# S5 in a decoder layer: a third accumulator bank, input copies by state tile, gates moved around the GLU, and the magnitudes and turns of the scan on VectorE in fewer, longer passes

## The chip, the cores and the metric

The kernel runs on one core of one Trainium2 chip. The metric is the device time of one execution in microseconds. Before the change the median of 3 runs is 1166.55 us (1165.32 to 1167.05).

## The reference, cut to what matters

One layer of a decoder over 288 tokens (256 of a prompt, and 8 samples of 4 new tokens each). One input projection feeds three branches and three sets of merge gates. Branch A is the one that the change is about: a diagonal complex state-space model (S5), then GELU, then a GLU.

```python
proj = x @ w_in                                   # 2048 -> xa, ga, ub, vb, gb, qkv, a, b, gate_c, zg
# branch A, 64 groups of 16 channels, 64 complex states each
bu = einsum('gpc,btgc->btgp', bb, u)              # bb from lam, dt, B
s  = associative_scan(s_t = a * s_(t-1) + bu_t)   # a = mag * exp(i * theta), complex
y  = Re(C s) + d * xa
z  = gelu(y);  z = z * sigmoid(z @ w_glu + b_glu)
pa = (z * silu(ga)) @ w_pa
g_a, g_b, g_c = sigmoid(zg + b_gate)
out = (g_a * pa + g_b * pb + g_c * pc) @ w_out
y = layernorm(ALPHA * x + out)
```

## The kernel before

All activations lie transposed, channels on partitions and 288 token columns along a row. Each weight matrix is streamed from memory once, in 322 pieces ("halves") of 128 x 1024 numbers. Each piece is loaded by SyncE's queue (`raw`), rounded to a high part on ScalarE (`wh`, line 203) and split from it on VectorE (`wl`, line 204 through the helper at line 136); `raw`, `wh` and `wl` have 3 buffers each. A product in full accuracy is three matmuls (high by high, low by high, high by low), so one half is 24 matmuls of 288 columns, all recorded at line 230.

The projections are jobs in a first-in-first-out list. `fill(n)` emits n units of 12 matmuls of that list, and the program calls it between the steps of the other work, so TensorE's order is the order of the calls. The other engines' orders are made by a scheduler; `tc.high_priority()` lifts some instructions ahead. Each job accumulates in one PSUM bank of the pool `ps_mm` (2 banks). The bank is free again when the job's result has been read: for a merge gate by the ScalarE tanh at line 1051 (`mth`), for a branch product by a VectorE pass.

S5 is worked in 8 blocks (n) of 128 channels, and each block in 4 state tiles (q) of 128 states. A state tile goes through these steps:

- `turn`, once per block: 16 small DMAs spread the block's input, split in a high part `uh` and a low part `ul`, over the partitions of `us` (one buffer for all 4 state tiles); two groups of 4 transposes go through a bank of their own (`wtp`), and ScalarE copies them to `ws`.
- `inputs(q)`: two matmuls into `bu` (real and imaginary part, 2 buffers of 2 banks).
- `phases`, for two state tiles at a time: tables of sine (`sn`) and cosine (`cn`) by ScalarE, with four copies of 40 columns for the samples.
- `states(q)`: ScalarE makes `am`, a row of 296 magnitudes with zeros where a sequence starts (line 1274, helper line 150; 2 buffers). VectorE turns `bu` by the tables (2 products of 592 columns, 2 sums of 296), POOL writes the start states into it (line 1284), VectorE scans real and imaginary part (line 1286) and turns back (2 products, 2 sums).
- `outputs`, for two state tiles at a time: 8 matmuls into `y5` (line 1303), then, after the second, the GELU (`gelu`: ScalarE and VectorE by turns).

Work that is not S5 is interleaved by the `fill` calls. At the end of S5 the GLU (8 jobs of one half, from `zh` and `zl`) follows in TensorE's order, then 16 `pa` products from `yah` and `yal`, with the merge gates of branch A among them. The first three of these gates stand ahead of S5 in the job list.

PSUM has 8 banks: 2 for `ps_mm`, 4 for `bu`, and one each for `wtp` and `y5` during S5. Names in the profile: L136, L140, L142 and L145 are the helpers `tt`, `ts` (one and two operations) and `stt`, and L150 is `copy`.

Of the kernel before, what the change touches and what calls it, by code (L numbers as in the profile page):

```python
# [79 lines left out]

LONG = ("ident", "m296", "iota", "iota16", "one", "mean")
_CW = {}


def constants():
# [36 lines left out]
    add("one", np.ones((P, P)))  # L122
    add("mean", np.full((P, P), 1.0 / P))
    return [np.ascontiguousarray(np.concatenate(x, 1)) for x in parts]
# [5 lines left out]
def body(tc, A):  # L130
# [124 lines left out]
    def project(n, done):  # L255
# [3 lines left out]
        ], done)  # L259

    def fill(n=1):
        while n and (jobs or now[0]):
            if now[0] is None:
                now[0] = run(ps_mm.tile([P, TT], F32, name="mm", tag="mm"), *jobs.popleft())
            if next(now[0], 0) == 0:
                now[0] = None
            else:
                n -= 1
# [78 lines left out]
    first = [ps_mm.tile([P, TT], F32, name="mm", tag="mm"), ps_mm.tile([P, TT], F32, name="mm", tag="mm"),  # L347
             psx.tile([P, 512], F32, name="mx", tag="a")[:, 0:TT]]
# [685 lines left out]
    mt = tc.alloc_tile_pool(name="mt", bufs=2, side="right")  # L1034
    mt3 = tc.alloc_tile_pool(name="mt3", bufs=3, side="right")
    s5 = tc.alloc_tile_pool(name="s5", bufs=1, side="right")

# [36 lines left out]
    def merge_gate(m):  # L1074
        def done(ps):
            gates[m] = mt3.tile([P, TT], F32, name="mga", tag="mga")
            with tc.high_priority():
                act(out=gates[m], in_=ps, func=AF.Tanh, scale=0.5, bias=bgate[:, 0, m:m + 1])
        project(ZG[m], done)
# [3 lines left out]

    lam = s5.tile([P, 3, 32], F32, name="lam")
    nc.sync.dma_start(out=lam, in_=A["lam"])
    dd = s5.tile([P, 8], F32, name="dd")
# [10 lines left out]
    mag = s5.tile(W32, F32, name="mag")  # L1097
    pre = tc.alloc_tile_pool(name="pre", bufs=1, side="right")

    def w32(name):  # L1100
# [49 lines left out]
    def frac_table(p_, iota):  # L1150
        q_ = pre.tile([P, 32, 16], F32, name="fq", tag="fq")
        io = mid(C(iota), 32)
# [50 lines left out]
    pss = tc.alloc_tile_pool(name="pss", bufs=1, space=PSUM, side="right")  # L1203
    psb = tc.alloc_tile_pool(name="psb", bufs=2, space=PSUM, side="right")

    class Block:


        def __init__(self, n):
# [21 lines left out]
            self.s = {}  # L1231

        def turn(self):
            self.us = s5.tile([P, 4, TX], F32R, name="us", tag="us")
            for q in range(4):
                for k, src in enumerate(self.u):
                    nc.sync.dma_start(out=self.us[32 * k:32 * k + 32, q].bitcast(F32), in_=src[32 * q:32 * q + 32].bitcast(F32))
            self.ws = s5.tile([P, 8, P], F32R, name="ws", tag="ws")
            for q in range(2):
                if q:  # L1240
                    fill(2)
                wp = pss.tile([P, 4, P], F32, name="wtp", tag="wtp")
                for k in range(4):
                    T.transpose(out=wp[:, k], in_=w4[:, 4 * q + k].rearrange("p b g c -> p (b g c)"), identity=ident)
                S.copy(out=self.ws[:, 4 * q:4 * q + 4], in_=wp)

        def inputs(self, q):
            self.bu = psb.tile([P, 2, 512], F32, name="bu", tag="bu")
            for ri in range(2):
                product(self.bu[:, ri, 0:TX], self.ws[:, 2 * q + ri], self.us[:, q], True, True)  # L1250

        def phases(self, q):
# [6 lines left out]
            tt(ph.rearrange("p n (a b) -> p n a b", a=16), i0, i1, add)  # L1259
            sn = s52.tile([P, 2, TX], F32, name="sn", tag="sn")  # L1260
            cn = s52.tile([P, 2, TX], F32, name="cn", tag="cn")
            act(out=pk, in_=ph, func=AF.Abs, bias=hp[:, 1:2])
            act(out=ph, in_=ph, func=AF.Abs)
            for a_, tb in ((pk, sn), (ph, cn)):
                act(out=a_, in_=a_, func=AF.Abs, bias=hp[:, 2:3])
                act(out=tb[:, :, 0:TP], in_=a_, func=AF.Sin, scale=TURN, bias=hp[:, 3:4])
                for i in range(2):
                    copy(tb[:, i, TP:].rearrange("p (b t) -> p b t", t=5), mid(tb[:, i, 0:5], 8))
            self.sn, self.cn = sn, cn

        def states(self, q):
            ti = 4 * self.n + q
            bu = self.bu
            cb = mid(self.cn[:, q % 2], 2)
            sb = mid(self.sn[:, q % 2], 2)
            am = tmp.tile([P, TX], F32, name="am", tag="s2")
            copy(am, C("m296"), mag[:, ti:ti + 1])
            z = s53.tile([P, 2, TX], F32, name="z", tag="z")
            u = s5.tile([P, 2, TX], F32, name="u", tag="u")
# [8 lines left out]
            u = s5.tile([P, 2, TX], F32, name="u", tag="u")  # L1288
            tt(u, z, sb, mult)
            tt(z, z, cb, mult)  # L1290
            tt(z[:, 0], z[:, 0], u[:, 1], sub)
            tt(z[:, 1], z[:, 1], u[:, 0], add)
# [43 lines left out]
    for n in range(8):  # L1336
        nxt = None
        for q in range(4):
# [25 lines left out]
    while done_["c"] < 16:  # L1364
        fill(2)
    psb.release()
    pss.release()
# [38 lines left out]
    def merge_a(m):  # L1406
# [11 lines left out]
    drain()  # L1418
    mt3.release()
    mt.release()  # L1420
# [48 lines left out]
    sh = psl.tile([P, 512], F32, name="sh", tag="sh")  # L1469
    T.matmul(sh[:, 0:TT], lhsT=C("mean"), rhs=ho[:, 0], start=True, stop=True)  # L1470
    copy(shift, sh[:, 0:TT])
    tt(ho[:, 0], ho[:, 0], shift, sub)
# [154 lines left out]
```

## Time and profile before

| | |
|---|---|
| median of 3 runs | 1166.55 us |
| the profiled execution | 1166.29 us, its span 1164.2 us |
| TensorE (PE) busy | 1125.4 us, 97% |
| VectorE (DVE) busy | 906.3 us, 78% |
| ScalarE (ACT) busy | 616.0 us, 53% |
| GpSimd (POOL) busy | 104.3 us, 9% |
| S5, first product of `bu` to the last `zh` | 534.9 to 902.2 us of the span |

The shares are averages over the whole span. Stages are read with a table of windows, in which each engine's busy time stands for a stretch. A matmul's duration in the profile (0.29 us) is its latency; in an undisturbed row the next one starts 0.12 us later. In the same way a VectorE instruction's duration overlaps the next one's start a little.

### The profile page before, as it was taken

What the parts mean: (1) busy time and instruction counts of PE and PEld (TensorE: products, weight loads), DVE (VectorE), ACT (ScalarE), POOL (GpSimd) and SP (SyncE); (2) the same over time, 40 slices, a digit from 0 to 9 for tenths busy, and PEclk for the clock granted to TensorE, in tenths of its full rate; (3) what the DMA queues carried; (4) which work ended last, traced back from release to release, by engine and by line L of the source; (5) the groups of instructions that cost most, each with busy time, mean ns of one, the idle gap of its engine ahead of it and who ended that gap; (6) DMA issues with size and microseconds to landing.
All of it is one profiled execution on the core that took longest, in us unless ns stands there. A gap on an engine that the chain in (4) does not pass through costs nothing.

```text
span 1164.2 us, 25793 instructions
## 1 busy us (share of the span) xinstructions
PE 1125.4 (97%) x10375; PEld 1084.8 (93%) x10375; DVE 906.3 (78%) x1634; ACT 616.0 (53%) x1020; POOL 104.3 (9%) x232
## 2 busy tenths in 40 slices
PE   8999999999999999999999999999999999999995
PEld 7998999999999999999999889889988999999994
DVE  5779656665365989878999999999998755557775
ACT  6665455444364344485666666566653444445553
POOL 0332212100010100000120000000101000000002
PEclk9999999999999999999999999999999999999997
DMA  9453444333374775655646455545455455555542
GB/s 327 148 164 113 144 135 156 121 120 110 126 277 153 260 258 168 182 186 176 185 151 200 159 165 174 173 161 176 152 173 182 157 181 181 181 181 170 179 161 82
DMA packets 68647, 199.24 MB, mean 171 GB/s; under 512 B 10992, under 2 KB 22544, under 8 KB 68400
## 3 DMA queue, kind: packets, MB, share of 16 engines
q1 hardware_dynamic: 67008, 192.12, 50.7%
q0 software_dynamic: 1520, 5.48, 1.2%
q8 instruction: 82, 1.34, 0.5%
q14 instruction: 37, 0.30, 0.1%
HBM read 184.09 MB, written 7.84 MB: 165 GB/s over the span
## 4 chain that ended last, share of the span: by engine, by line
PE 67%; DVE 19%; issue 4%; ACT 3%; DMA 3%; POOL 0%; SPq 0%; ACTq 0%; POOLq 0%; DVEq 0%
PE mm L230 58%; DVE wl L136 7%; DVE z L136 4%; DVE u L136 2%; DVE z L1286 2%; DMA raw<-in_wst 1%; ACT wh L203 1%; PE up L616 1%; PE wp L610 1%; PE a L626 1%; DMA cT<-in_cT 1%; DMA s<-in_s 1%; PE a L602 0%; PE y L1303 0%; POOL z L1284 0%
## 5 line engine op out<-in xcount | busy, mean ns | idle before, releaser
L230 PE MATMUL mm<-xh,wh 128*128 128x288 f32 x1872 | 545.7, 292 | 10.0 <-ACT mth L1051 9.2
L230 PE MATMUL mm<-xh,wl 128*128 128x288 f32 x1872 | 536.3, 286 | 0.0
L230 PE MATMUL mm<-xl,wh 128*128 128x288 f32 x1872 | 536.1, 286 | 0.0
L136 DVE TENSOR_TENSOR wl<-raw,wh 128x1024 fp32r<-128x1024 f32 x322 | 393.3, 1222 | 150.8 <-ACT wh L203 143.5
L203 ACT CAST wh<-raw 128x1024 fp32r<-128x1024 f32 x322 | 335.2, 1043 | 320.0 <-PE mm L230 281.7
L230 PEld LDWEIGHTS mm<-xh,wh 128*128 128x128 f32 x1872 | 354.3, 189 | 23.4 <-ACT mth L1051 11.8
L230 PEld LDWEIGHTS mm<-xl,wh 128*128 128x128 f32 x1872 | 354.6, 189 | 0.3
L230 PEld LDWEIGHTS mm<-xh,wl 128*128 128x128 f32 x1872 | 354.5, 189 | 0.0
L230 PE MATMUL mm<-mh,wh 128*128 128x288 f32 x256 | 73.4, 287 | 0.0
L230 PE MATMUL mm<-ml,wh 128*128 128x288 f32 x256 | 73.2, 286 | 0.0
L230 PE MATMUL mm<-mh,wl 128*128 128x288 f32 x256 | 73.2, 286 | 0.0
L136 DVE TENSOR_TENSOR z<-z,u 128x296 f32<-128x296 f32 x128 | 55.1, 464 | 0.6
L1286 DVE TENSOR_TENSOR_SCAN z<-am,z 128x296 f32<-128x296 f32 x64 | 46.9, 764 | 4.3 <-POOL z L1284 2.8
L230 PEld LDWEIGHTS mm<-ml,wh 128*128 128x128 f32 x256 | 48.4, 189 | 0.1
L230 PEld LDWEIGHTS mm<-mh,wh 128*128 128x128 f32 x256 | 48.4, 189 | 0.1
L230 PEld LDWEIGHTS mm<-mh,wl 128*128 128x128 f32 x256 | 48.4, 189 | 0.0
L145 DVE SCALAR_TENSOR_TENSOR cy<-cb,convw,cy 128x312 f32<-128x312 f32 x72 | 38.3, 539 | 8.5 <-ACT cy L384 7.3
L150 ACT ACTIVATE am<-cst,mag 128x296 f32<-128x296 f32 x32 | 17.3, 542 | 47.1 <-DVE z L1286 47.1
L230 PE MATMUL mm<-yah,wh 128*128 128x288 f32 x128 | 36.7, 287 | 0.5 <-DVE yah L1396 0.5
L230 PE MATMUL mm<-ybh,wl 128*128 128x288 f32 x128 | 36.7, 287 | 0.4 <-DVE wl L136 0.4
L230 PE MATMUL mm<-ybh,wh 128*128 128x288 f32 x128 | 37.1, 290 | 0.0
L230 PE MATMUL mm<-ych,wh 128*128 128x288 f32 x128 | 37.1, 290 | 0.0
(443 smaller groups left out, 1702.6 us busy)
## 6 DMA issues: line engine op xcount, KB each, us to landing
raw<-in_wst SPq DMA_DIRECT2D x322, 512.0 KB, 3.4
s<-in_s SPq DMA_DIRECT2D x8, 512.0 KB, 6.0
out_delta_s<-s POOLq DMA_DIRECT2D x8, 512.0 KB, 3.5
r<-in_wst SPq DMA_DIRECT2D x7, 384.0 KB, 7.4
us<-uh SPq DMA_DIRECT2D x64, 37.0 KB, 3.2
us<-ul SPq DMA_DIRECT2D x64, 37.0 KB, 3.2
vu<-in_xT SPq DMA_DIRECT2D x7, 288.0 KB, 7.4
out_y<-ho SPq DMA_DIRECT2D x8, 144.0 KB, 2.1
```

The costliest lines, as they stand in the source:

```text
L136: (eng or V).tensor_tensor(out=out, in0=a, in1=b, op=op)
L145: V.scalar_tensor_tensor(out=out, in0=a, scalar=s, in1=b, op0=op0, op1=op1)
L150: act(out=out, in_=a, func=AF.Copy, scale=scale)
L203: S.copy(out=h, in_=r)
L230: T.matmul(pairs(ps), lhsT=w, rhs=paired(x), start=start, stop=stop)
L610: T.matmul(wp[R, h4], lhsT=xt[R, h4], rhs=r[R, h4], start=True, stop=True)
L616: T.matmul(up[:, h4], lhsT=kd[R, h4], rhs=w[R, h4], start=True, stop=True)
L626: T.matmul(a[Q, h4], lhsT=nb[R, h4, 1], rhs=w[R, h4], start=(c == 0 and h4 == 0), stop=True, skip_group_check=True)
L1286: V.tensor_tensor_scan(out=z[:, ri], data0=am, data1=z[:, ri], initial=0.0, op0=mult, op1=add)
```

## The change

- The job list gets three accumulator banks during S5: `mm_bank()` goes round `ps_mm`, `ps_mm` and a new pool `psm`. The bank comes from `wtp`: the transposes of `turn` now take a bank from the same round. After S5 the job list is back at two banks.
- `us` is four tiles, one per state tile. Two of them are spread when the block is made, the other two in `turn`.
- `am` is made by VectorE (a multiplication by a scalar per partition) instead of ScalarE.
- `sn` and `cn` are one tile `tab`, and `bu` or `z` is multiplied by both tables in one pass of 1184 columns instead of two of 592. The four small copies per pair of state tiles are one.
- One of the `fill` calls of the odd blocks emits 4 units instead of 5, so 4 units of the job list stand later. S5 ends with the job at hand finished, so that `psm` can be given back.
- Gate 3 of branch A, which stood behind the first `pa` product, stands between the GLU and the first `pa`; each later gate moves with it, into a new pool of 6 buffers.
- Constants: `iota` and `iota16` are loaded where they are used and given back; `mean` is `one` with a scale of 1/128 in the copy behind it; `lam` lies in the pool of the preparation.

```diff
-LONG = ("ident", "m296", "iota", "iota16", "one", "mean")
+LONG = ("ident", "m296", "one")
...
+    mm_pools = [ps_mm]
+    def mm_bank():
+        mm_pools.append(mm_pools.pop(0))
+        return mm_pools[-1].tile([P, 512], F32, name="mm", tag="mm")
...
-                now[0] = run(ps_mm.tile([P, TT], F32, name="mm", tag="mm"), *jobs.popleft())
+                now[0] = run(mm_bank()[:, 0:TT], *jobs.popleft())
...
-            gates[m] = mt3.tile([P, TT], F32, name="mga", tag="mga")
+            gates[m] = mtg[m > 2].tile([P, TT], F32, name="mga", tag="mga")
...
+    psm = tc.alloc_tile_pool(name="psm", bufs=1, space=PSUM, side="right")
+    mm_pools[:] = [ps_mm, ps_mm, psm]
...
+            self.us = {}
+            self.spread(0)
+            self.spread(1)
+        def spread(self, q):
+            self.us[q] = s5.tile([P, TX], F32R, name="us", tag="us%d" % q)
+            for k, src in enumerate(self.u):
+                nc.sync.dma_start(out=self.us[q][32 * k:32 * k + 32].bitcast(F32), in_=src[32 * q:32 * q + 32].bitcast(F32))
         def turn(self):
-            self.us = s5.tile([P, 4, TX], F32R, name="us", tag="us")
-            for q in range(4):
-                for k, src in enumerate(self.u):
-                    nc.sync.dma_start(out=self.us[32 * k:32 * k + 32, q].bitcast(F32), in_=src[32 * q:32 * q + 32].bitcast(F32))
+            self.spread(2)
+            self.spread(3)
...
-                wp = pss.tile([P, 4, P], F32, name="wtp", tag="wtp")
+                wp = mm_bank().rearrange("p (k c) -> p k c", k=4)
...
-                for i in range(2):
-                    copy(tb[:, i, TP:].rearrange("p (b t) -> p b t", t=5), mid(tb[:, i, 0:5], 8))
+            copy(t4[:, :, TP:].rearrange("p k (b t) -> p k b t", t=5),
+                 t4[:, :, 0:5].rearrange("p k (o t) -> p k o t", o=1).to_broadcast([P, 4, 8, 5]))
+        def products(self, x, q):
+            pr = s5.tile([P, 2, 2, TX], F32, name="pr", tag="pr")
+            tt(pr, x.rearrange("p i (o t) -> p i o t", o=1).to_broadcast([P, 2, 2, TX]),
+               self.tab[:, q % 2].rearrange("p (o j) t -> p o j t", o=1).to_broadcast([P, 2, 2, TX]), mult)
+            return pr
...
-            copy(am, C("m296"), mag[:, ti:ti + 1])
+            ts(am, C("m296"), mag[:, ti:ti + 1])
-            tt(z, bu[:, :, 0:TX], cb, mult)
-            tt(u, bu[:, :, 0:TX], sb, mult)
-            tt(z[:, 0], z[:, 0], u[:, 1], add)
-            tt(z[:, 1], z[:, 1], u[:, 0], sub)
+            pr = self.products(self.bu[:, :, 0:TX], q)
+            tt(z[:, 0], pr[:, 0, 0], pr[:, 1, 1], add)
+            tt(z[:, 1], pr[:, 1, 0], pr[:, 0, 1], sub)
...
-                fill(((3, 3), (4, 5), (3, 2), (4, 2))[q][n % 2])
+                fill(((3, 3), (4, 4), (3, 2), (4, 2))[q][n % 2])
...
+    while now[0] is not None:
+        fill()
+    mm_pools[:] = [ps_mm]
+    psm.release()
...
+    mtg.append(tc.alloc_tile_pool(name="mt6", bufs=6, side="right"))
+    merge_gate(3)
     for m in range(16):
         merge_a(m)
-        if m < 13:
-            merge_gate(m + 3)
+        if m < 12:
+            merge_gate(m + 4)
```

VectorE's queue in one state tile of the second block, before; `wl` is the split of a weight half and `merged` a merge of another branch:

```order
L136 TENSOR_TENSOR z<-bu,cn 128x592
L136 TENSOR_TENSOR u<-bu,sn 128x592
L136 TENSOR_TENSOR wl<-raw,wh 128x1024
L136 TENSOR_TENSOR z<-z,u 128x296 x2
L145 SCALAR_TENSOR_TENSOR merged<-mth,mm 128x288
L1286 SCALAR_TENSOR_TENSOR z<-am,z 128x296 x2
L136 TENSOR_TENSOR wl<-raw,wh 128x1024
L136 TENSOR_TENSOR u<-z,sn 128x592
L136 TENSOR_TENSOR ph<-fu,fv 128x512
L136 TENSOR_TENSOR z<-z,cn 128x592
```

And the same state tile in the changed kernel:

```order
L135 TENSOR_TENSOR pr<-bu,tab 128x1184
L135 TENSOR_TENSOR wl<-raw,wh 128x1024
L135 TENSOR_TENSOR z<-pr 128x296 x2
L1309 SCALAR_TENSOR_TENSOR z<-am,z 128x296
L144 SCALAR_TENSOR_TENSOR merged<-mth,mm 128x288
L1309 SCALAR_TENSOR_TENSOR z<-am,z 128x296
L135 TENSOR_TENSOR wl<-raw,wh 128x1024
L135 TENSOR_TENSOR pr<-z,tab 128x1184
L139 TENSOR_SCALAR am<-cst_205,mag 128x296
L135 TENSOR_TENSOR z<-pr 128x296 x2
```

Two products have become one, and the row of magnitudes of a later state tile stands in the queue as one more pass. Over S5 (first product to last `zh`) the queue holds 565 instructions before and 531 after.

TensorE's queue where S5 ends, before; `y` is the last output of S5, `xh` the last unit of the job list ahead of it, `zh` and `zl` the GLU:

```order
L230 MATMUL mm<-xl,wh 128x288
L230 MATMUL mm<-xh,wl 128x288
L1303 MATMUL y_11861<-z,cT 32x296 x4
L230 MATMUL mm<-zh,wh 128x288
L230 MATMUL mm<-zl,wh 128x288
```

And after:

```order
L229 MATMUL mm<-xh,wl 128x288
L1324 MATMUL y_11704<-z,cT 32x296 x4
L229 MATMUL mm<-xh,wh 128x288
L229 MATMUL mm<-xl,wh 128x288
L229 MATMUL mm<-xh,wl 128x288
```

One unit (12 matmuls) of the job list now stands between the last output and the GLU. Between the first `bu` of the last block and the last output stand 33 units instead of 31. In the same way, 4 units of gate 3 now stand between the last matmul of the GLU and the first `mm<-yah`.

## Rows read from the trace of the kernel before

**Rows 1.** The page, part 1: busy us, share of the span, instructions.

```profile
PE 1125.4 (97%) x10375; PEld 1084.8 (93%) x10375; DVE 906.3 (78%) x1634; ACT 616.0 (53%) x1020; POOL 104.3 (9%) x232
```

**Rows 2.** Busy time by stretch: stretch, length, PE, PEld, DVE, ACT, POOL, PEclk, DMA.

```profile
534.90:851.10 316.20, 304.87 (x2421) 290.98 (x2421) 309.26 (x492) 197.28 (x342) 32.29 (x82) 0.99 0.53 168
875.00:902.20 27.20, 26.20 (x209) 24.20 (x207) 23.56 (x36) 10.80 (x14) 4.35 (x7) 1.00 0.58 188
840.00:870.00 30.00, 27.55 (x209) 26.48 (x209) 29.65 (x50) 13.46 (x25) 3.85 (x9) 0.94 0.56 177
```

**Rows 3.** Waits of PE, 534 to 903 us: us in total, times, longest.

```profile
PE mm L230 <- ACT mth L1051: 8.8, 9, 1.8
PE bu L230 <- DMA us<-ul: 2.4, 1, 2.4
PE mm L230 <- DVE zh L1381: 1.3, 1, 1.3
```

**Rows 4.** Waits of DVE, same stretch.

```profile
DVE wl L136 <- ACT wh L203: 3.9, 4, 1.5
DVE z L1286 <- POOL z L1284: 2.8, 7, 0.4
```

**Rows 5.** Waits of ACT, same stretch.

```profile
ACT am L150 <- DVE z L1286: 47.1, 26, 5.9
```

**Rows 6.** The chain that ended last, 834 to 850 us: start, us, what.

```profile
837.63 1.13 DVE wl L136
...
843.57 2.53 DMA us<-ul
...
846.67 3.46 PE mm L230 x18
```

**Rows 7.** Groups by form: busy us, mean ns of one; idle before.

```profile
L136 DVE TENSOR_TENSOR z<-z,u 128x296 f32<-128x296 f32 x128 | 55.1, 464 | 0.6
L136 DVE TENSOR_TENSOR z<-bu,cn 128x592 f32<-128x592 f32 x32 | 24.6, 770 | 0.1
L142 DVE TENSOR_SCALAR gw<-gw 128x296 f32<-128x296 f32 x8 | 2.5, 309 | 0.0
L142 DVE TENSOR_SCALAR vn<-vn,mv,vy 128x1024 f32<-128x1024 f32 x2 | 1.6, 799 | 0.0
L150 ACT ACTIVATE am<-cst,mag 128x296 f32<-128x296 f32 x32 | 17.3, 542 | 47.1 <-DVE z L1286 47.1
```

**Rows 8.** DVE in order of time, 835 to 905 us: start, us, instruction.

```profile
848.57 0.77 DVE L136 TENSOR_TENSOR z<-z,cn 128x592 f32<-128x592 f32 x1
849.26 1.22 DVE L136 TENSOR_TENSOR wl<-raw,wh 128x1024 fp32r<-128x1024 f32 x1
...
862.75 0.31 DVE L142 TENSOR_SCALAR gw<-gw 128x296 f32<-128x296 f32 x1
862.98 0.77 DVE L136 TENSOR_TENSOR z<-bu,cn 128x592 f32<-128x592 f32 x1
...
888.11 0.77 DVE L136 TENSOR_TENSOR u<-bu,sn 128x592 f32<-128x592 f32 x1
888.91 0.84 DVE L136 TENSOR_TENSOR z<-z,u 128x296 f32<-128x296 f32 x2
```

**Rows 9.** PE in order of time: start, us, instruction, idle before it and releaser.

```profile
846.18 0.49 PE L230 MATMUL bu<-us,ws 128*128 128x296 f32 x2 [2.45 <-DMA us<-ul]
...
847.76 0.45 PE L230 MATMUL mm<-xh,wh 128*128 128x288 f32 x1
848.00 0.45 PE L230 MATMUL mm<-xl,wh 128*128 128x288 f32 x1
...
850.40 0.45 PE L230 MATMUL mm<-xh,wl 128*128 128x288 f32 x1
...
902.53 0.39 PE L230 MATMUL mm<-zh,wh 128*128 128x288 f32 x1 [1.33 <-DVE zh L1381]
...
927.27 0.39 PE L230 MATMUL mm<-yah,wh 128*128 128x288 f32 x1 [0.46 <-DVE yah L1396]
```

More of the change, by code (lines that the diff above doesn't have):

```diff
@@ L122, in constants @@
     add("one", np.ones((P, P)))
-    add("mean", np.full((P, P), 1.0 / P))
     return [np.ascontiguousarray(np.concatenate(x, 1)) for x in parts]
@@ L346, in body @@
     tc.keep_in_program_order(nc.sync.dma_start(out=wab, in_=A["wab"]))
-    first = [ps_mm.tile([P, TT], F32, name="mm", tag="mm"), ps_mm.tile([P, TT], F32, name="mm", tag="mm"),
+    first = [ps_mm.tile([P, 512], F32, name="mm", tag="mm")[:, 0:TT], ps_mm.tile([P, 512], F32, name="mm", tag="mm")[:, 0:TT],
              psx.tile([P, 512], F32, name="mx", tag="a")[:, 0:TT]]
@@ L1035, in body @@
     mt3 = tc.alloc_tile_pool(name="mt3", bufs=3, side="right")
+    mtg = [mt3]
     s5 = tc.alloc_tile_pool(name="s5", bufs=1, side="right")
@@ L1082, in body @@
         merge_gate(m)
-    lam = s5.tile([P, 3, 32], F32, name="lam")
-    nc.sync.dma_start(out=lam, in_=A["lam"])
     dd = s5.tile([P, 8], F32, name="dd")
@@ L1098, in body @@
     pre = tc.alloc_tile_pool(name="pre", bufs=1, side="right")
+    lam = pre.tile([P, 3, 32], F32, name="lam")
+    nc.sync.dma_start(out=lam, in_=A["lam"])
+    iotas = {}
+    for name in ("iota", "iota16"):
+        _, o_, w_ = _CW[name]
+        iotas[name] = pre.tile([P, w_], F32, name=name)
+        nc.sync.dma_start(out=iotas[name], in_=A["cst1"][:, o_:o_ + w_])
     def w32(name):
@@ L1151, in frac_table @@
         q_ = pre.tile([P, 32, 16], F32, name="fq", tag="fq")
-        io = mid(C(iota), 32)
+        io = mid(iotas[iota], 32)
         tt(p_, b3(hi, 16), io, mult)
@@ L1249, in inputs @@
             for ri in range(2):
-                product(self.bu[:, ri, 0:TX], self.ws[:, 2 * q + ri], self.us[:, q], True, True)
+                product(self.bu[:, ri, 0:TX], self.ws[:, 2 * q + ri], self.us[q], True, True)
         def phases(self, q):
@@ L1259, in phases @@
             tt(ph.rearrange("p n (a b) -> p n a b", a=16), i0, i1, add)
-            sn = s52.tile([P, 2, TX], F32, name="sn", tag="sn")
-            cn = s52.tile([P, 2, TX], F32, name="cn", tag="cn")
+            tab = s52.tile([P, 2, 2, TX], F32, name="tab", tag="tab")
             act(out=pk, in_=ph, func=AF.Abs, bias=hp[:, 1:2])
             act(out=ph, in_=ph, func=AF.Abs)
-            for a_, tb in ((pk, sn), (ph, cn)):
+            for j, a_ in ((1, pk), (0, ph)):
                 act(out=a_, in_=a_, func=AF.Abs, bias=hp[:, 2:3])
-                act(out=tb[:, :, 0:TP], in_=a_, func=AF.Sin, scale=TURN, bias=hp[:, 3:4])
-                for i in range(2):
-                    copy(tb[:, i, TP:].rearrange("p (b t) -> p b t", t=5), mid(tb[:, i, 0:5], 8))
@@ L1269, in phases @@
-            self.sn, self.cn = sn, cn
+                act(out=tab[:, :, j, 0:TP], in_=a_, func=AF.Sin, scale=TURN, bias=hp[:, 3:4])
+            t4 = tab.rearrange("p i j t -> p (i j) t")
+            copy(t4[:, :, TP:].rearrange("p k (b t) -> p k b t", t=5),
+                 t4[:, :, 0:5].rearrange("p k (o t) -> p k o t", o=1).to_broadcast([P, 4, 8, 5]))
+            self.tab = tab
+        def products(self, x, q):
[3 more added lines that the diff above has]
+            return pr
@@ L1271, in states @@
         def states(self, q):
             ti = 4 * self.n + q
-            bu = self.bu
-            cb = mid(self.cn[:, q % 2], 2)
-            sb = mid(self.sn[:, q % 2], 2)
             am = tmp.tile([P, TX], F32, name="am", tag="s2")
-            copy(am, C("m296"), mag[:, ti:ti + 1])
+            ts(am, C("m296"), mag[:, ti:ti + 1])
             z = s53.tile([P, 2, TX], F32, name="z", tag="z")
-            u = s5.tile([P, 2, TX], F32, name="u", tag="u")
-            tt(z, bu[:, :, 0:TX], cb, mult)
@@ L1286, in states @@
                 V.tensor_tensor_scan(out=z[:, ri], data0=am, data1=z[:, ri], initial=0.0, op0=mult, op1=add)
[L1288 to L1292, printed above, removed]
+            pr = self.products(z, q)
+            tt(z[:, 0], pr[:, 0, 0], pr[:, 1, 1], sub)
+            tt(z[:, 1], pr[:, 0, 1], pr[:, 1, 0], add)
             G.tensor_copy(out=sst[:, ti, :, 0:1], in_=z[:, :, TP - 1:TP])
@@ L1412, in merge_a @@
         queue([(("pa", m, 0), lambda k: yah[:, k], lambda k: yal[:, k])], done)
+    mtg.append(tc.alloc_tile_pool(name="mt6", bufs=6, side="right"))
+    merge_gate(3)
     for m in range(16):
         merge_a(m)
-        if m < 13:
-            merge_gate(m + 3)
+        if m < 12:
+            merge_gate(m + 4)
     drain()
+    mtg[1].release()
     mt3.release()
@@ L1469, in body @@
     sh = psl.tile([P, 512], F32, name="sh", tag="sh")
-    T.matmul(sh[:, 0:TT], lhsT=C("mean"), rhs=ho[:, 0], start=True, stop=True)
-    copy(shift, sh[:, 0:TT])
+    T.matmul(sh[:, 0:TT], lhsT=C("one"), rhs=ho[:, 0], start=True, stop=True)
+    copy(shift, sh[:, 0:TT], 1.0 / P)
     tt(ho[:, 0], ho[:, 0], shift, sub)
```

## The prediction

> **What bounds the kernel now.** I read the page's busy shares first. TensorE (PE) is busy 97% of the span and VectorE (DVE) 78% [rows 1], so over the whole kernel PE sets the time, and a change can win only what PE waits. That average hides the stage that the diff touches. The windows show it: from the first product of S5 to the start of its last block, 534.9 to 851.1 us, DVE is busy 309.3 of 316.2 us, while PE shows 304.9 and ACT 197.3 [rows 2]. In S5 two engines are full at once, and a gain on one is worth only what the other allows.
>
> The table of waits says what PE waits for there: 8.8 us in nine pieces for the tanh `mth` on ACT, which gives an accumulator bank back; 2.4 us once for the `us` copies; 1.3 us for `zh` where the GLU starts [rows 3]. ACT is not short of time, but its queue is in order, and `am` stands in it waiting 47.1 us for the scan on DVE to free a buffer [rows 5]; a tanh behind it is late with it. The chain of waits confirms that this goes back to DVE: before 843 us it runs through DVE's splits and turns, at 843.57 it passes over the `us` copy, which had stood in SP's queue behind a weight load that waited for DVE's split, and from 846.67 it is PE's own [rows 6]. So up to about 843 us DVE's queue sets the pace, and from there to the GLU PE's.
>
> DVE itself has little to give back: it waits 3.9 us for `wh`, 2.8 us for POOL's start states [rows 4], and little else by name; the rest of its 6.9 idle us [rows 2] is short gaps between dependent passes.
>
> **The change part by part.** DVE's queue up to the last block comes first (7 blocks, 28 state tiles).
>
> Passes. Two of 592 columns become one of 1184, twice per state tile, so 56 instructions go. A pass of 592 lasts 0.770 us and one of 296 0.464 [rows 7]: 1.034 ns a column. A pass of 592 is followed after 0.69 us (848.57 to 849.26 [rows 8]), of which the columns are 0.61; what is saved per instruction is about 0.075 us. 56 x 0.075 = 4.2 us less. The bounds are 0 (nothing saved) and the whole difference of the durations, 0.770 - 0.612 = 0.158, which is 8.8 us; I take the start-to-start figure, since DVE is back to back here.
>
> The Trainium skill ("VectorE: DVE Perf Modes", The DRAIN you can't avoid) says that the next operation doesn't issue until the pipe is empty, so that only the count of operations matters. By that the saving would be the 8.8 us, and the kernel some 4 us faster than I forecast. The rows overlap by 0.08 us and speak against it. No run here shows a pass of 1184.
>
> Magnitudes. DVE gets 32 passes of 296 columns with one scalar per partition; in the queue 2 of them stand before the first product and 28 between it and the last block. The nearest row is `gw`, the same size: 0.309 us, the next one starting 0.23 later [rows 7, 8]. A pass with two scalars per partition, `vn`, takes 0.799 for 1024 columns [rows 7]; at half of 1.034 ns a column `gw` would make 0.685 of that, so a scalar may cost 0.057 more, and `am` 0.29. If it ran one column at a time it would be the 0.464 row, 0.38 start to start. I take 0.23: 28 x 0.23 = 6.4 us more (bounds 6.4 and 10.6; below, nothing, where it falls into a gap).
>
> Splits. Because one `fill` is shorter, the queue holds 89 `wl` in these blocks instead of 91. The chain gives 1.13 us for one [rows 6]: 2.3 us less.
>
> Gaps. A sum right behind the product that it reads costs 0.80 instead of 0.69 (888.11 to 888.91 [rows 8]), 0.11 us. Counted in the queues over all of S5, such pairs fall from 18 to 6, and a turn right behind its scan from 11 to 7: 16 x 0.11 x 28/32 = 1.5 us less. A scan right behind its sums, with POOL between, stands 9 times instead of 7, at 0.4 [rows 4]: 0.7 more. ACT loses `am` (0.54 us each [rows 7]) and with it the wait on DVE, and its casts come sooner; about half of the 3.9 us [rows 4] lies here, and I let 2.0 go (bounds 0 and 3.9).
>
> DVE's line: -4.2 + 6.4 - 2.3 - 1.5 + 0.7 - 2.0 = -2.9 us at the start of the last block.
>
> The 8.8 us for `mth` are not in this sum. The third bank and the freed ACT queue take this wait away, and then the next thing that is late is the split of the weights, since DVE's queue is no shorter than I count it. They count only if DVE was not the limit (first rival). That the transposes share the round of banks costs PE nothing: three banks leave two for jobs while ACT copies one, what there was before.
>
> Copies. The first matmul of the last block waited 2.45 us for `us` (846.18 [rows 9]). Its copies are now issued a half block earlier into tiles of their own: -2.4. The copies stay in SP's queue among the weight loads; if they are still late, this term is 0.
>
> Behind that wait the granted clock fell: 0.94 in the window from 840 to 870 [rows 2], the lower of the two levels, 1.2 instead of 2.4 GHz. Matmuls started 0.24 apart from 847.5 to 850.6 instead of 0.12 (847.76, 848.00, 850.40 [rows 9]), half of some 3 us: -1.5, if PE has no such pause.
>
> From the first `bu` of the last block PE sets the time. Two more units stand before the last output, 24 matmuls x 0.1225 = +2.9. One more stands between it and the GLU, +1.5, and lies where PE waited 1.3 for `zh` [rows 3], +0.2 net.
>
> GLU to `pa`. PE waited 0.46 us for `yah` (927.27 [rows 9]); 4 units of a gate now stand there, 5.9 us of work: -0.5. This work is taken from later, so it costs nothing; the same gates are computed.
>
> At nothing: the constants (two loads of 16 columns and `lam`, in a stretch where DVE has other work queued), the scale of the mean (an instruction with the same columns), the tables' copies (ACT is idle for over a third of this stretch [rows 2]), the pool of 6 gates.
>
> Sum: -2.9 - 2.4 - 1.5 + 2.9 + 0.2 - 0.5 = -4.2. Against the profiled execution's own 1166.29 us that is 1162.1; this execution lies 0.3 below the median, so the forecast is 1162, rounded.
>
> **The rivals.**
>
> PE set free. If DVE's queue was full only because it ran ahead of its work, all that PE waits goes: 8.8 + 2.4 + 1.3 [rows 3] + 0.5 + 1.5 of clock = 14.5 us, 1152. For it speaks that PE is nowhere recorded as waiting for a split or a turn in S5. Against it speaks that DVE idles 2% and its work doesn't shrink. Chance 0.18.
>
> No change. The copies still arrive late, or `am` costs 0.29 and no gap closes: DVE's line is -4.2 + 8.1 - 2.3 = +1.6, and with the copies, the clock, the units and the GLU the end moves by 1.6 - 2.4 - 1.5 + 2.9 + 0.2 - 0.5 = +0.3, 1167. Chance 0.14.
>
> Slower: the moved magnitudes are more than a full DVE can hide. Place: DVE's queue in S5. It decides from the point where DVE's line grows by 1.3 us, 0.05 per state tile, because the two added units ahead of the last output then meet a PE that is no earlier. Price: at 0.38 the line is -4.2 + 10.6 - 2.3 + 0.7 = +4.8, the end +3.5, 1170; with passes that save nothing, 1174. For it speaks the full DVE; against it, that `gw` and `vn` both run at two columns a cycle [rows 7]. I give it 1170 and a chance of 0.11.
>
> The Trainium skill ("Perfetto Trace Analysis", Optimizing Scalar/DVE Operations) says that where VectorE is saturated, offloading to ScalarE may make sense; the change does the reverse. By that rule the sign would be this rival's. The trace agrees that VectorE is full, but also shows ACT's copy of the work blocking its queue for 47.1 us [rows 5].
>
> **How the numbers follow.** Chances: the forecast 0.57, PE set free 0.18, no change 0.14, slower 0.11. A measurement of this kernel tells about 0.2%, 2.3 us, from no change, so faster means under 1164.2 and slower over 1168.9. The forecast's own spread (`am` at 0.29: +1.7; passes from 0 to 8.8: +4.2 to -4.6; `wh`: +2.0 to -1.9) is 1157 to 1167; I put 0.09 of its 0.57 above 1164.2, and 0.01 of the no-change case beyond 1168.9. Faster: 0.48 + 0.18 = 0.66; same: 0.09 + 0.13 = 0.22; slower: 0.11 + 0.01 = 0.12. The range reaches to PE set free and short of the slower case: 1152 to 1168.
>
> **What the profile after would show.** Right: DVE still over 97% busy in S5; a pass of 1184 columns at 1.38 us (0.158 + 1184 x 1.034 ns), followed after 1.30; `am` at about 0.31; no PE wait for `mth` or `us`, and instead PE waits for `wl` or `z`; no stretch at the lower clock; the GLU starting some 4 us earlier. Wrong: DVE under 95% in S5 with PE free of waits (then PE set free); `am` over 0.4 or passes over 1.5 (slower); a wait for `us` that stays (no change).

## The result, and the profile after

The changed kernel takes 1172.84 us (median of 4 runs, 1171.97 to 1175.03) beside 1166.8 us for the kernel before (4 runs): a ratio of 1.0065, 95% interval 1.0052 to 1.0078. (All ratios in this document are the recorded estimates, which differ a little from the quotient of the two medians, here 1.0052.) It is slower by 6 us where 4 us less were forecast, and the time lies outside the range. The profiled execution, the slowest of the four, took 1175.03 us with a span of 1173.2.

The page's busy shares of the changed kernel [rows 1]: the work is nearly the same, PE 4.7 us more, DVE 2.9 more, ACT 17.9 less.

```profile
PE 1130.1 (96%) x10375; PEld 1089.7 (93%) x10375; DVE 909.2 (77%) x1602; ACT 598.1 (51%) x940; POOL 109.0 (9%) x232
```

Its windows [rows 2]: from the first product of S5 to the start of the last block, and two stretches of 30 us.

```profile
536.20:854.50 318.30, 302.02 (x2363) 287.35 (x2363) 308.88 (x461) 179.26 (x268) 34.78 (x84) 0.98 0.50 166
840.00:870.00 30.00, 24.54 (x174) 23.41 (x174) 27.51 (x42) 16.26 (x26) 2.24 (x8) 0.89 0.39 135
750.00:780.00 30.00, 25.56 (x189) 24.67 (x190) 28.06 (x45) 19.13 (x30) 1.92 (x7) 0.89 0.44 149
```

The first stretch is 2.1 us longer than before, not 2.9 shorter; DVE is busy 97% of it (98% before). In the two short ones PE is idle for more than 4 us and its granted clock falls to 0.89.

What PE waits for, 534 to 913 us [rows 3]:

```profile
PE mm L229 <- ACT gaS L1048: 5.5, 1, 5.5
PE mm L229 <- ACT mth L1058: 5.4, 1, 5.4
PE mm L229 <- DVE wl L135: 3.5, 7, 1.2
PE mm L1265 <- ACT mth L1058: 1.7, 1, 1.7
```

The nine waits for `mth` have become one of 5.4 us, one of 5.5 us for `gaS` (ScalarE's silu of `ga`, which gives back a bank in the same way), and one of 1.7 us in front of a group of transposes (line 1265). The one for `us` is gone, and PE waits for splits (`wl`) 7 times. What DVE waits for [rows 4]:

```profile
DVE wl L135 <- ACT wh L202: 8.6, 7, 1.7
DVE z L1309 <- POOL z L1307: 3.2, 8, 0.4
DVE pr L135 <- PE bu L229: 2.3, 2, 1.6
```

The 8.6 us for `wh` are not to be set beside the 3.9 of [rows 4], since most of them lie behind the start of the last block. From the first product to there (534.9 to 851.1 us before, 536.2 to 854.5 after):

```profile
DVE wl L136 <- ACT wh L203: 3.0, 3, 1.5
DVE wl L135 <- ACT wh L202: 3.1, 3, 1.5
```

There the wait neither grew nor shrank.

And ACT [rows 5]: the 47.1 us of `am` are gone, but its queue waits for DVE elsewhere, at the tables (`tab`, 21.3 us) and at their phases (`pk`, 17.2).

```profile
ACT tab L1286 <- DVE pr L135: 21.3, 10, 3.7
ACT pk L1282 <- DVE ph L135: 17.2, 11, 4.2
```

The groups by form [rows 7], 534 to 913 us; then DVE in order of time at two places [rows 8].

```profile
L135 DVE TENSOR_TENSOR pr<-z,tab 128x1184 f32<-128x1184 f32 x32 | 44.3, 1385 | 0.2
L135 DVE TENSOR_TENSOR pr<-bu,tab 128x1184 f32<-128x1184 f32 x32 | 44.2, 1382 | 2.3 <-PE bu L229 2.3
L139 DVE TENSOR_SCALAR am<-cst,mag 128x296 f32<-128x296 f32 x30 | 10.9, 366 | 0.0
```

```profile
748.16 0.37 DVE L139 TENSOR_SCALAR am<-cst,mag 128x296 f32<-128x296 f32 x1
748.45 0.68 DVE L135 TENSOR_TENSOR ph<-fu,fv 128x512 f32<-128x512 f32 x1
...
854.53 1.39 DVE L135 TENSOR_TENSOR pr<-bu,tab 128x1184 f32<-128x1184 f32 x1 [1.64 <-PE bu L229]
855.84 1.22 DVE L135 TENSOR_TENSOR wl<-raw,wh 128x1024 fp32r<-128x1024 f32 x1
```

The pass of 1184 columns takes 1.38 us and is followed after 1.31, as forecast. `am` takes 0.366 us and is followed after 0.29: the value for a scalar per partition that was worked out and not taken.

PE in order of time at the longer wait [rows 9], and ACT over the same stretch (start, us, instruction, idle before it):

```profile
842.01 0.60 PE L1265 MATMUL mm<-cst,w 128*128 128x128 f32 x4
848.08 0.61 PE L229 MATMUL mm<-xh,wh 128*128 128x288 f32 x1 [5.46 <-ACT gaS L1048]
848.48 0.45 PE L229 MATMUL mm<-xl,wh 128*128 128x288 f32 x1
848.72 0.45 PE L229 MATMUL mm<-xh,wl 128*128 128x288 f32 x1
...
854.00 0.50 PE L229 MATMUL bu<-us,ws 128*128 128x296 f32 x2
```

```profile
831.65 1.05 ACT L202 CAST wh<-raw 128x1024 fp32r<-128x1024 f32 x1
836.91 0.72 ACT L1282 ACTIVATE pk<-ph,hp 128x512 f32<-128x512 f32 x1 [4.21 <-DVE ph L135]
...
842.89 0.72 ACT L1282 ACTIVATE pk<-ph,hp 128x512 f32<-128x512 f32 x1 [0.39 <-DVE ph L135]
843.52 1.03 ACT L202 CAST wh<-raw 128x1024 fp32r<-128x1024 f32 x1
844.45 0.58 ACT L1266 CAST ws<-mm 128x512 fp32r<-128x512 f32 x1
...
847.62 0.40 ACT L1048 ACTIVATE gaS<-mm 128x288 f32<-128x288 f32 x1
```

A chain over three engines can be read here. ACT stands 4.21 us before `pk`, whose phase `ph` comes late in DVE's queue. Then it works without a pause of any size for 11 us on two pairs of tables, and the copy of the transposes (made on PE from 838.63, copied at 844.45) and `gaS` stand behind them. PE's next job is to have the bank that `gaS` reads, since the two groups of transposes have taken the two other places of the round, and PE waits 5.46 us. After that wait the 24 matmuls from 848.08 to 853.76 start 0.24 apart instead of 0.12 (granted clock 0.89 in the window): another 2.9 us.

Why `ph` comes late can be read from DVE's queue. DVE makes 16 of these phases, each for two state tiles. In the changed kernel the 7th, 11th and 15th stand behind the first products of 11, 19 and 27 state tiles; before, it was 9, 17 and 25. Each of them now comes right in front of the next one, so ACT gets two pairs of tables at one place, three times, and each time a block's transposes stand there too. Two of the three places are those of the long PE waits, and the third is that of the 1.7 us. The 15th and 16th phase in the changed kernel, and then in the kernel f17 below, in which ACT makes `am` again:

```profile
836.21 0.67 DVE L135 TENSOR_TENSOR ph<-fu,fv 128x512 f32<-128x512 f32 x1
842.16 0.69 DVE L135 TENSOR_TENSOR ph<-fu,fv 128x512 f32<-128x512 f32 x1
...
799.98 0.68 DVE L135 TENSOR_TENSOR ph<-fu,fv 128x512 f32<-128x512 f32 x1
827.10 0.69 DVE L135 TENSOR_TENSOR ph<-fu,fv 128x512 f32<-128x512 f32 x1
```

The order is the scheduler's. Of all kernels traced here only those with `am` on DVE have phases so close (5 to 7 us from the end of one to the start of the next): e1 and e4 at the same three places, e3 at two, e5 at one.

Counted along PE, before against after: the first matmul of the last block comes at 846.18 and 854.00 (+7.8), from there to the GLU 52.2 and 55.0 (+2.8), from there to the first `pa` 25.7 and 30.7 (+5.0), from there to the end 240.1 and 233.5 (-6.6). The loss lies before the last block.

### The profile page after: what moved, and what is told of

Read it like the earlier page. It is cut to its first block, busy times and chain, and to the rows that moved or that the text cites. A ratio compares the mean times of both kernels' runs of the same rounds, so it can differ in the third digit from the quotient of the medians.

```text
span 1173.2 us, 25669 instructions
## 1 busy us (share of the span) xinstructions
PE 1130.1 (96%) x10375; PEld 1089.7 (93%) x10375; DVE 909.2 (77%) x1602; ACT 598.1 (51%) x940; POOL 109.0 (9%) x232
## 4 chain that ended last, share of the span: by engine, by line
PE 62%; DVE 19%; issue 11%; ACT 2%; DMA 2%; POOL 1%; SPq 0%; DVEq 0%; POOLq 0%; ACTq 0%
PE mm L229 54%; DVE wl L135 6%; DVE pr L135 4%; DVE z L135 2%; DVE z L1309 2%; ACT wh L202 1%; DMA raw<-in_wst 1%; PE up L622 1%; PE wp L616 1%; PE a L632 1%; PE y L1324 1%; POOL z L1307 1%; DVE ho L135 1%; PE a L608 0%; PE pp L562 0%
## 5 line engine op out<-in xcount | busy, mean ns | idle before, releaser
L135 DVE TENSOR_TENSOR z<-pr 128x296 f32<-128x296 f32 x128 | 54.6, 459 | 0.2
L135 DVE TENSOR_TENSOR pr<-bu,tab 128x1184 f32<-128x1184 f32 x32 | 44.2, 1382 | 2.3 <-PE bu L229 2.3
L135 DVE TENSOR_TENSOR pr<-z,tab 128x1184 f32<-128x1184 f32 x32 | 44.3, 1385 | 0.2
L229 PE MATMUL mm<-ych,wl 128*128 128x288 f32 x128 | 37.8, 296 | 0.4 <-DVE wl L135 0.4
L1314 POOL COPY sst<-z 128x2 f32<-128x2 f32 x32 | 20.5, 640 | 188.6 <-DVE z L135 188.6
```

The costliest lines, as they stand in the source:

```text
L135: (eng or V).tensor_tensor(out=out, in0=a, in1=b, op=op)
L229: T.matmul(pairs(ps), lhsT=w, rhs=paired(x), start=start, stop=stop)
```

## Experiments

Besides ratios (to runs of the kernel before on the same chip) one number of each trace is used, called **the stretch**: the time on DVE from the first product of the first block to the first product of the last, 316.2 us before and 318.3 after. Kernels that start from the one before also load the constants and end S5's last job as the change does.

In the quoted texts of e1 to e4, theory A puts the cost in the round of banks, B and C in VectorE's part (magnitudes, passes, one table). In e5 and e6, B is VectorE's longer queue and D the one table for both products. From e9 on the letters are new, and explained there.

**Which part costs.** e1: the changed kernel with a bank of its own for the transposes and two for jobs. e4: three banks, but both groups of a block's transposes in one.

```diff
-    mm_pools[:] = [ps_mm, ps_mm, psm]                                  # e1
...
-                wp = mm_bank().rearrange("p (k c) -> p k c", k=4)      # e1, e4
+                wp = pss.tile([P, 4, P], F32, name="wtp", tag="wtp")   # e1
...
+            own = mm_pools.pop(0)                                      # e4: one bank for both groups
...
+                wp = own.tile([P, 512], F32, name="mm", tag="mm").rearrange("p (k c) -> p k c", k=4)
...
+            mm_pools.append(own)
```

> The changed kernel with one part undone: the transposes of turn get a bank of their own again and the job list goes back to two banks. Theory A (the transposes in the round of banks give the next job the bank of the job just ended, so that TensorE waits for ScalarE's queue): the waits of 5.5, 5.4 and 1.7 us at three turns and the two drops of the clock behind them go, 1157 to 1163 us. Rival B (VectorE carries more: the magnitudes): no part of VectorE's work is touched, 1170 to 1174. Rival C (one table tile makes ScalarE wait for VectorE's pass, 21 us): also untouched, 1170 to 1174.

> The changed kernel with three banks still shared, but both groups of transposes of a block in the same one, so that the next job gets the third bank and not that of the job just ended. A: as e1 or better, 1156 to 1163. B and C: 1170 to 1174. If the number of banks itself is the trouble and not which bank, it stays at 1170 to 1174 as well while e1 is fast.

Measured: e1 1168.44, ratio 1.0026 (1.0014 to 1.0039); e4 1168.13, 1.0020 (1.0009 to 1.0031). Both lie between the theories: the round costs some 0.4% here, and something else 0.2 to 0.3%. PE's waits of e4, 534 to 910 us:

```profile
PE mm L1267 <- ACT ws L1268: 7.9, 3, 3.0
PE mm L230 <- DVE wl L135: 2.6, 6, 1.1
PE mm L230 <- ACT mth L1059: 1.2, 1, 1.2
```

The wait for a job's bank is gone, but now the second group of transposes waits three times, up to 3.0 us, for ACT's copy of the first (in e1 too: three times, 7.3 us in all). ACT is late in the changed kernel, in e1 and in e4.

e2: the kernel before with the round of three banks alone. e3: before with VectorE's part alone (magnitudes on VectorE, one table, passes of 1184).

```diff
+    mm_pools[:] = [ps_mm, ps_mm, psm]                  # e2
...
-            copy(am, C("m296"), mag[:, ti:ti + 1])     # e3
+            ts(am, C("m296"), mag[:, ti:ti + 1])
...
+            pr = self.products(self.bu[:, :, 0:TX], q)
```

> The kernel before with the round of three banks alone (copies of the input, magnitudes, passes, gates and fill counts as before; the constants as in the changed kernel). A: slower than before, 1171 to 1180, with PE waits of several us behind the second group of transposes. B and C: 1160 to 1167, since the third bank can only help.

> The kernel before with VectorE's part alone: magnitudes on VectorE, one table, passes of 1184 columns; two banks for jobs and one for the transposes. A: 1160 to 1167, no wait of more than 2 us at a turn. B and C: slower than before, 1170 to 1175.

Measured: e2 1168.73, 1.0020 (1.0007 to 1.0033), between the theories. Its trace has no bank wait of several us; the last block's first matmul comes 1.0 us later than before, and most of the rest lies behind S5 (from the GLU to the first `pa` 27.9 us instead of 25.7, at a granted clock of 0.95 from 898 to 930 us, 1.00 before). e3 1173.15, 1.0066 (1.0051 to 1.0081), as B and C expected: VectorE's part alone costs as much as the whole change.

**Which half of VectorE's part.** e5: before with the magnitudes on VectorE. e6: before with one table and the passes of 1184.

> The kernel before with the magnitudes on VectorE alone (two tables, passes of 592 columns). Theory B (VectorE's queue is full, 30 passes of 0.28 us start to start are 8.4 us more for it): 1171 to 1175. Theory D (the cost of e3 comes from the one table: ScalarE stands 21 us waiting to write it, the casts of the weights behind it come late, and VectorE waits 10 us for them): 1165 to 1169, since ScalarE loses its 47 us of waits for the scan.

> The kernel before with one table and passes of 1184 columns alone; the magnitudes stay on ScalarE. Theory B: VectorE has 4.4 us less work, 1161 to 1165. Theory D: 1169 to 1175, with ScalarE waiting some 20 us for VectorE's pass at the table.

Measured: e5 1170.6, 1.0032 (1.0017 to 1.0046); e6 1167.28, 1.0010 (0.9999 to 1.0021). Neither text holds: the magnitudes cost less than B said, and the passes, 4.4 us less work for DVE, gain nothing by themselves. In e6 the saving turned into waits of DVE, 534 to 910 us:

```profile
DVE z L1308 <- POOL z L1306: 5.0, 12, 0.5
DVE wl L135 <- ACT wh L202: 3.7, 4, 1.2
DVE pr L135 <- PE bu L229: 3.2, 2, 2.2
```

That is 2.2 us more for POOL [rows 4], and 3.2 for `bu`, for which it had not waited.

**The rest.** e7: the changed kernel without VectorE's part and with two banks and `wtp` (so: copies by state tile, units, gates). e8: e7 with e4's three banks.

> The changed kernel without its VectorE part and without the round of banks: what is left is the input copies by state tile, the gates around the GLU and the shorter fill. If the parts add up (e1 is 4.7 us faster than e3, from these three), 1166.2 - 4.7 = 1161.5 us, 1159 to 1164, without a PE wait for us and with half a us or less at zh. If they were only worth it because VectorE was overfull, 1164 to 1168.

> As e7 with three banks, both groups of transposes of a block in one of them. If PE's waits for the tanh are what a third bank takes away and nothing else takes their place, 3 to 6 us faster than e7, 1156 to 1160. If VectorE's queue holds PE anyway (splits come late instead), within 2 us of e7.

Measured: e7 1165.51, 0.9992 (0.9979 to 1.0004), no gain that can be told from none; e8 1165.01, 0.9985 (0.9974 to 0.9997), a small one. Both second texts hold.

**The price of VectorE's time.** e9 adds a pass to DVE and leaves `am` on ACT; e10 takes `am` from ACT and gives it to GpSimd; e11 does the same to e8, and e12 gives GpSimd the `am` that DVE has in e4.

```diff
+            ts(s5.tile([P, TX], F32, name="dum", tag="dum"), z[:, 0], mag[:, ti:ti + 1])   # e9
...
-            copy(am, C("m296"), mag[:, ti:ti + 1])                                         # e10, e11 (e12: from ts on DVE)
+            ts(am, C("m296"), mag[:, ti:ti + 1], eng=G)
```

> The kernel before with one pass more on VectorE per state tile: a multiplication of 296 columns by a scalar per partition whose result nobody reads, the same form as the magnitudes of the changed kernel (0.28 us start to start there). The magnitudes themselves stay on ScalarE. 32 such passes are 9.0 us of VectorE's time. Theory D (VectorE's time alone made e5 slower): as slow as e5, 1169 to 1172. Theory E (e5 gained by the free ScalarE queue and lost more by VectorE's pass): slower than e5, 1173 to 1176. Theory F (e5 was slow because ScalarE's wait moved to its tables): 1166 to 1168, the pass falls into VectorE's gaps.

> The kernel before with the magnitudes made by GpSimd instead of ScalarE: 32 passes taken from ScalarE, none given to VectorE. Theory D (VectorE's time is e5's cost): not slower than before, 1163 to 1167. Theory E: faster, 1160 to 1164, since the freed queue now comes free of charge. Theory F (the freed ScalarE queue runs into waits for tables that are in use, and this is e5's cost): 1169 to 1171, as e5. A price that is open: a pass on GpSimd may delay its start states and so VectorE's scans; VectorE's waits for GpSimd (2.8 us before) would show it.

> e8 (three banks with both groups of transposes in one bank, input copies by state tile, gates around the GLU; VectorE's part as before) with the magnitudes on GpSimd. Theory D: as e8, 1164 to 1166. Theory E: faster than e8 by 2 to 4 us, 1161 to 1163. Theory F: 1168 to 1170.

> The whole changed kernel, but with the transposes in one bank and the magnitudes on GpSimd: VectorE has the passes of 1184 columns and no magnitudes, so some 4 us less work than before. Theory D and E: 1160 to 1164, since the passes' saving now stays. If the passes save nothing by themselves, as in e6: 1165 to 1167. Theory F: 1168 to 1170.

Measured: e9 1173.74, 1.0072 (1.0060 to 1.0084), as theory E expected: 9.0 us of DVE's time cost 8.1 us. The stretch grew by 6.6 us, to 322.8, though PE had nothing to do with the pass, and `ph` stands in DVE's queue where it stood before. e10 1171.2, 1.0044 (1.0031 to 1.0058); e11 1170.79, 1.0046 (1.0032 to 1.0060), both near theory F; e12 1167.12, 1.0012 (1.0004 to 1.0021), at the time given for passes that save nothing; yet beside e11, which lacks them, e12 is 3.7 us faster. No one theory holds for e9 and e10 together, but it does not pay to take `am` from ACT even where DVE is not given it. In e10 a pass on GpSimd took 2.0 us, and one of DVE's four products, which often runs beside it, grew from 0.772 to 0.831 on average; the other three stayed within 0.006 of before:

```profile
L139 POOL TENSOR_SCALAR am<-cst,mag 128x296 f32<-128x296 f32 x32 | 63.9, 1998 | 80.6 <-DVE z L1312 62.2 <-DVE mag L144 16.7 <-DVE cT L139 1.6
L135 DVE TENSOR_TENSOR z<-z,cn 128x592 f32<-128x592 f32 x32 | 26.6, 831 | 0.5
```

**What was still open.** f13: e4 with the magnitudes back on ACT (passes of 1184 kept). f14: e9's pass on GpSimd. f15: before with the copies by state tile alone. f16: f15 with e4's banks.

> e8 (three banks with both groups of transposes in one bank, input copies by state tile, gates around the GLU; magnitudes on ScalarE) with the passes of 1184 columns, so some 4 us less of VectorE's work and nothing given to it. PE waited for VectorE's splits 9 times in e8 (5.4 us). If VectorE's time is what is left in e8: 1160 to 1163. If the one table that ScalarE must fill for both products takes the saving back, as in e6: 1164 to 1168.

> e9's pass more per state tile, but on GpSimd: 32 passes of some 2 us there, none taken from ScalarE or VectorE. If GpSimd's passes are what made e10 slow (VectorE's turns lasted 0.83 instead of 0.77 us beside them): slower than before by as much or more, 1170 to 1175. If e10 was slow by ScalarE's waits for its tables: not slower, 1165 to 1168.

> The kernel before with the input copies by state tile alone. By the prediction's term: the wait of 2.4 us for the copies goes, and the lower clock behind it, 1162 to 1164. If VectorE's line sets the time up to there: 1165.5 to 1167, and a wait for a split or a tanh in the place of the copies' wait.

> f15 with three banks, both groups of transposes in one bank: e8 without the moved units and gates. If these are worth what the prediction said (two units more before the last output, a gate taken from later: no net gain), it is within 1.5 us of e8: 1163.5 to 1166.5. If the moved gates pay: 1166.5 to 1169.

Measured: f13 1164.01, 0.9977 (0.9968 to 0.9986), where its second text begins, and not to be told from e8. f14 1168.04, 1.0016 (1.0006 to 1.0025): GpSimd's passes cost 1.8 us, a third of the 5.6 that e10 lost, so neither of its texts holds whole; they took 1.6 us each there, and none of DVE's four products was longer on average. f15 1166.38, 1.0001 (0.9993 to 1.0010): PE's wait for the copies went, the last block's first matmul came 1.2 us earlier, but from there to the GLU it took 53.9 us instead of 52.2; the stretch was 316.4 us and the end the same. f16 1166.14, 1.0004 (0.9996 to 1.0013): the first text holds, and e8's moved units and gates are worth 0.2% at most (the two intervals just meet).

**One line undone.** f17 is the changed kernel with nothing but this:

```diff
-            ts(am, C("m296"), mag[:, ti:ti + 1])
+            copy(am, C("m296"), mag[:, ti:ti + 1])
```

> The changed kernel with the magnitudes back on ScalarE, and nothing else changed. f13 has this with the transposes in one bank (ratio 0.9977). If the two costs add: the round's 0.45% on top of f13, 1168 to 1170, with PE waits of some 5 us for a result in the bank of the job just ended. If the round costs only where ScalarE's queue holds table work in the place of the magnitudes: 1163 to 1166, and no such wait over 3 us.

Measured: 1163.2 (12 runs, 1161.91 to 1165.95), 0.9973 (0.9963 to 0.9983), the lowest median of all. The second text holds: with `am` on ACT the round of banks costs nothing that shows (f13 has the other banks and 0.9977); with it on DVE the round costs 0.45% (1.0065 against e4's 1.0020, which has the phases at the same places). f17's window to the last block, and its waits of PE and ACT, 534 to 900 us:

```profile
534.10:844.90 310.80, 301.85 (x2395) 287.70 (x2394) 302.29 (x435) 191.43 (x297) 40.87 (x83) 0.99 0.50 168
```

```profile
PE mm L229 <- DVE wl L135: 4.2, 9, 0.9
PE mm L229 <- ACT ws L1266: 2.4, 1, 2.4
PE mm L229 <- ACT mth L1058: 2.0, 1, 2.0
PE mm L229 <- ACT gaS L1048: 0.9, 1, 0.9
...
ACT am L149 <- DVE z L1309: 47.2, 26, 4.1
...
ACT tab L1286 <- DVE pr L135: 8.4, 9, 1.2
ACT pk L1282 <- DVE ph L135: 7.7, 7, 2.2
```

The stretch is 7.5 us shorter than in the changed kernel. ACT waits as long at `am` as it did before the change (47.2 us [rows 5]), and PE does not mind. ACT's queue at the 16th phase of f17, which stands right in front of the last block's transposes there:

```profile
827.83 0.72 ACT L1282 ACTIVATE pk<-ph,hp 128x512 f32<-128x512 f32 x1 [0.96 <-DVE ph L135]
...
833.75 0.58 ACT L1266 CAST ws<-mm 128x512 fp32r<-128x512 f32 x1
835.39 1.05 ACT L202 CAST wh<-raw 128x1024 fp32r<-128x1024 f32 x1 [1.06 <-PE mm L229]
836.34 0.40 ACT L1048 ACTIVATE gaS<-mm 128x288 f32<-128x288 f32 x1
```

The phase in front of it, the 15th, came at 800 us here and at 836 in the changed kernel. So ACT has one pair of tables to make at this place instead of two, and `ws` and `gaS` are out early enough that PE waits 0.9 us and not 5.46.

f17 undoes two things by its one line: the pass on DVE, and the late phases that the scheduler's order brought with it. No run has the one without the other in the changed kernel, so how the 9.6 us divide between DVE's time and the order is not shown. e9, in which the order of `ph` stayed, shows what DVE's time alone can cost in the kernel before.

## Why the prediction was wrong

Two steps failed. The first is the move of the magnitudes: the prediction gave it +6.4 us of DVE's time and -2.0 of waits for `wh`, together +4.4, and said that PE would lose nothing by the shared banks; undone, it gives back 9.6 us (1172.84 to 1163.2; the two profiled executions lie 12.9 apart). In place of these terms the runs show 8.4 us of DVE's time, waits for `wh` that stayed, and late phases that held ACT, and through its banks PE, twice for 5.4 us. The second is the rest of the change, above all the copies and the clock. Without the move's terms the forecast would be 1157.7, and that kernel, f17, takes 1163.2. Of the 10.7 us by which 1172.84 misses 1162.1, the move thus makes 5.2 and the rest 5.5.

- **Passes: right on DVE's line, not at the end.** 1.38 us and followed after 1.31. Summed from start to next start over the stretch, the turns' products take 75.2 us instead of 80.1: -4.9, forecast -4.2. At the end that gave nothing in e6, nothing that can be told from none in f13 beside e8, and 3.7 us in e12 beside e11. The Trainium skill ("VectorE: DVE Perf Modes", The DRAIN you can't avoid) says that the next operation does not start until the pipe is empty, but also that one which is not held starts earlier; the prediction left that out. The trace agrees with the second: after a pass of 1184 the next one starts 0.07 us before its recorded end, and 56 passes fewer saved 4.9 us, not 8.8.
- **Magnitudes: mis-sized.** 28 take 8.4 us of the stretch (0.30 each), forecast 6.4, bounds 6.4 to 10.6. `gw`, which was taken, has no scalar per partition; the 0.29 worked out from `vn` was right. That is 2.0 of the 5.2 us.
- **Splits: right.** 89 instead of 91, their time 101.8 us instead of 104.3, forecast -2.3.
- **Waits for `wh`, -2.0: did not come.** Up to the last block they are 3.0 us before and 3.1 after, and 2.0 in f17, where ACT waits 47.2 us at `am` again. What ACT's queue gained it lost at `tab` (21.3 us, in f17 8.4) and at `pk` (17.2, in f17 7.7).
- **Gaps: right, as far as they can be told from the passes.** The turns' products, the sums and the scans together take 160.8 us instead of 166.6: -5.8, forecast -4.2 - 1.5 + 0.7 = -5.0. POOL's waits, which are in it, go from 2.4 to 3.2 us up to the last block.
- **DVE's line**: -5.8 + 8.4 - 2.5 = +0.1, and +2.1 in all, forecast -2.9; most of the remaining 2.0 is DVE's wait for the last block's `bu`, which PE's long wait had made late (1.64 us). The +2.1 is past the 1.3 us from which the third rival was said to decide: its sign, its place (DVE's queue) and, within 3 us, its time (1170) came true, though not by its price (`am` at 0.38; it is 0.30). In its place the late `ph` held ACT, and ACT held PE.
- **"The third bank and the freed ACT queue take this wait away": wrong.** The two long PE waits (5.37 and 5.46 us, with some 5 us more lost at the lower clock behind them) stand where the nine short ones were. What was read as an obstacle, `am` waiting in ACT's queue, had cost little (f17 has it again); what stood behind it depends on DVE too.
- **"That the transposes share the round of banks costs PE nothing": right only while ACT copies in time** (f17); with ACT late it costs 5 us (e4, 1168.13, against the changed kernel).
- **Copies, -2.4, and clock, -1.5: nothing.** These are 3.9 of the rest's 5.5 us. The wait went, but in f15 what PE gains ahead of the last block (1.2 us) is given back before the GLU (+1.7). So "from the first `bu` of the last block PE sets the time" does not hold either.
- **Two units more, +2.9: the sum fits, partly by luck.** From the last block to the GLU the terms are +2.9, +1.5 for the unit ahead of the GLU and -1.5 of clock, +2.9 together, and +2.8 was measured; but f15, without the units, has +1.7 there, and f17, with them, +4.6. **Gate units, taken from later: right** (+5.0 to `pa`, -6.6 behind it).

The Trainium skill ("Perfetto Trace Analysis", Optimizing Scalar/DVE Operations) says that offloading from a saturated VectorE to ScalarE may make sense, and by that rule the change had the wrong sign. The runs agree: f17, with `am` back on ScalarE, is 9.6 us faster. In e9 a microsecond more of VectorE's time costs 0.9 us of the end.

The stretch orders the kernels once they are put in two groups, since with the shorter fills 4 units of PE's work (some 5.9 us) stand behind the stretch instead of in it. With them: f17 and f13 310.8 (ratios 0.9973, 0.9977), e8 312.2 (0.9985), e7 312.3 (0.9992), e12 314.8 (1.0012), e4 316.6 (1.0020), e1 317.0 (1.0026), e11 317.1 (1.0046), the changed kernel 318.3 (1.0065). Without: f16 316.1 (1.0004), f15 316.4 (1.0001), e2 316.7 (1.0020), e6 317.3 (1.0010), f14 318.1 (1.0016), e5 319.4 (1.0032), e10 320.7 (1.0044), e9 322.8 (1.0072), e3 323.7 (1.0066). Only e2 stands well above its neighbours, and its loss lies in part behind S5; the other inversions (f16 and f15, e9 and e3) are within the intervals.

Three things are open: how f17's 9.6 us divide between DVE's time and the place of `ph`; why e5, with the same VectorE work added as e9, lost only half as much (`am` is independent of its neighbours and may fill gaps between dependent passes, where e9's pass reads the sums in front of it; DVE idles 4.9 us of e5's stretch and 6.4 of e9's, which points that way, but it was not tried); and what besides GpSimd's passes cost e10 its 5.6 us.

## What to carry to other kernels

A long wait in an engine's in-order queue is worth removing only if what stands behind it is needed and ready; list what comes next in that queue and what it waits for, since the wait may only move on and let other work pile up in front of something urgent. Where one engine is 98% busy over a stage, price a us given to it at half a us (e5) to nine tenths (e9) of the end, do not count on a us taken from it (e6), and test the one-line undo first: it separated 9.6 us here. Where a scheduler makes the order, compare the order before and after too: one added pass moved `ph` by two state tiles. A bank shared in a round cost nothing while the engine that empties it was early, and 5 us when it was late.

## What the runs showed of the hardware

- A multiplication of 296 columns by a scalar per partition took 0.366 us, one by constants 0.309 [rows 7]; on ScalarE 0.542, on GpSimd 2.0 (e10; 1.6 in f14).
- Beside a GpSimd pass some VectorE passes grew and others did not. In e10 a GpSimd pass ran from 604.68 to 607.27 us: the product that started at 606.38 took 1.00 us (0.77 alone), while the split in front of it, from 605.24, took its usual 1.22.
- After the two PE pauses of 5.37 and 5.46 us, 16 and 24 matmuls ran at the lower level, 0.24 us apart, which cost a third to a half of the pause again; after one of 0.89 us (f17) they started 0.12 apart as ever. The length of the pause does not settle it: after one of 2.45 us (before, 846.18) the level fell, after one of 2.43 (f17, 704.76) it did not.
